# A two-layer trunk whose instruction order comes from the framework's other engine model

## The chip, the cores and the metric

The kernel runs on one core of one Trainium2 chip. The metric is the device time of one execution in microseconds (us), as the median of several runs. The engines are PE (matrix products), DVE (VectorE), ACT (ScalarE), POOL (GpSimd) and SP (which here only issues transfers). A transfer can be issued by SP, ACT or POOL; those that add into their destination are all issued by POOL in this kernel.

## The reference

The reference is a causal decoder trunk with batch 1, 512 positions, width 1024 and two layers, all in float32:

```
x = x + dilated_attention_mixer(rmsnorm(x, g_a), w_qkv, w_out)   # 3 groups x 8 heads of 128
x = x + swiglu_ffn(rmsnorm(x, g_f0), w_gate_up[0], w_down[0])    # inner width 2816
x = x + pooling_mixer(rmsnorm(x, g_p), w_in, w_group, scale)     # windows 2, 4, 8, 16
x = x + swiglu_ffn(rmsnorm(x, g_f1), w_gate_up[1], w_down[1])
return rmsnorm(x, g_final)

def swiglu_ffn(h, w_gate_up, w_down):
    gate, up = split(h @ w_gate_up)
    return (silu(gate) * up) @ w_down
```

The attention has three groups with (window, dilation) of (128, 1), (512, 4) and (2048, 16). The outputs of the three groups are merged, head by head, by a softmax over their log-sums, and a projection follows.

## The kernel before

The activations lie with features on the 128 partitions and the 512 positions along the row: x is eight tiles of 128x512 (x_5528 to x_5535 in the program's numbering). Every product is made in split float32: a matrix is written as a rounded part and a remainder, and three matmuls stand for one (L329, L330 and L332 for plain products in `Product.add`; L461, L462 and L463 in `mult`; L632 to L634 in `values12`). Weights arrive by a transfer into a `raw` tile, then ACT copies the rounded part (L92) and DVE subtracts for the remainder (L93). In a few places, the `lean` loads, ACT writes the rounded part (L146) and its negative (L147), and a transfer by POOL adds the weight itself from memory (L149); so DVE has no part in them. The rings are short: 5 `w` tiles, 4 `raw`, 2 `half`, and all accumulators share the 8 banks of PSUM (`ps`).

Most of the large products are made by Strassen's scheme with seven products for eight. `seven` does it for queries, keys and values, `chained` for the two FFN layers, where three accumulators are reused and ACT copies each out (L535, L539, L543, L551) before the next group of matmuls starts. The sums of weight blocks that the scheme needs are made by DVE (L189, L190) from the `raw` tiles. Their results are put together by DVE (L502, L508, L515, L516 in `seven`; L664 to L677 in `values12`).

The attention runs head by head, and its pieces are hung between the products of the next head. For head h: `scores0` and `scores12` make the scores; `merge` computes the weight of each group on DVE in a chain of small steps (L771 to L781), multiplies the four score blocks `s0` on DVE (L783) and the four of `s12` on ACT (L786); `turn0` has PE transpose `s0` (L802), and ACT (L806, L808) and DVE (L809) put the result in `t0`; `turn12` does the same for `s12` (L823, L828); `output` multiplies with the values (L841, L847). L610 and L850 add or scale what PE has accumulated.

Between the sub-layers stands an RMSNorm. `note` scales each x tile for the next sub-layer (L393, L394), `square` squares it on ACT (L382) and adds the squares up on DVE (L384); `rstd` sums them with PE matmuls against ones (L411), then DVE (L414) and POOL (L417) take the power, and `spread` brings the row to all partitions with PE (L424). In the last FFN each down product is added to x (L1224, or L1361 for one half of the positions). The final norm is taken in two halves of the positions, each with its own `rstd`: of the first half the five late tiles are added (L1361), squared (L1363) and summed (L1402), then L1373 scales the eight tiles and they are written. Of the second half, tiles are scaled by the norm's weights first (L1389 on ACT, L1387 on DVE), turned by PE (L1397) and scaled by the power at the end (L1437, L1439).

**What sets the order.** The Python code emits the instructions in one sequence, in which the author has interleaved the stages by hand (a planner, `pump`, walks two queues of loads and weight splits ahead of the products, and lists of hooks hang attention steps between products). The tile framework takes this sequence, builds the dependences, and lets a scheduler choose the order in which each engine will issue its instructions. That scheduler walks a model of the engines in time. The program it emits is static: each engine issues its own list in order, and an instruction that is not ready holds up all those behind it on its engine, however ready these may be. Semaphores are put in for the order chosen. Which tile of a ring a new value gets follows from the sequence as well.

In the program before, PE's order is nearly the written one: counted over all pairs of PE instructions, 6 pairs stand the other way round.

## Time and profile before

| | before |
|---|---|
| time, median of 3 runs | 1186.43 us (1184.93 to 1186.91) |
| span of the profiled execution | 1184.0 us |
| PE busy | 1175.4 us (99%), 10042 matmuls |
| DVE busy | 989.0 us (84%) |
| ACT busy | 721.7 us (61%) |
| POOL busy | 171.3 us (14%) |
| transfers | 207.57 MB, mean 175 GB/s |

The profile is of one execution, and its times count from the start of the span. Busy time is what an engine spent in its instructions; matmuls overlap, so their own durations are longer than the distance from one start to the next. A row of the timeline has the start, the busy time, the engine, the line of the kernel, the operation, its output and inputs, their shapes, how many instructions were put together, and in brackets how long the engine stood idle before it and who ended that. The heads are numbered 0 to 7: up to about 475 us the core is in the attention, then to about 786 us in the first FFN, to about 860 us in the pooling layer, and then in the second FFN.

### The profile page before, as it was taken

What the parts mean: (1) busy time and instruction counts of PE and PEld (TensorE: products, weight loads), DVE (VectorE), ACT (ScalarE), POOL (GpSimd) and SP (SyncE); (2) the same over time, 40 slices, a digit from 0 to 9 for tenths busy, and PEclk for the clock granted to TensorE, in tenths of its full rate; (3) what the DMA queues carried; (4) which work ended last, traced back from release to release, by engine and by line L of the source; (5) the groups of instructions that cost most, each with busy time, mean ns of one, the idle gap of its engine ahead of it and who ended that gap; (6) DMA issues with size and microseconds to landing.
All of it is one profiled execution on the core that took longest, in us unless ns stands there. A gap on an engine that the chain in (4) does not pass through costs nothing.

```text
span 1184.0 us, 25180 instructions
## 1 busy us (share of the span) xinstructions
PE 1175.4 (99%) x10042; PEld 1119.9 (95%) x10042; DVE 989.0 (84%) x1733; ACT 721.7 (61%) x1262; POOL 171.3 (14%) x165
## 2 busy tenths in 40 slices
PE   9999999999999999999999999999999999999997
PEld 7889999999999989889999999988889999999997
DVE  7997898889789888699988988656789998898875
ACT  6554564546455557747756775775575766676553
POOL 1101111111111002311111111122130111111100
PEclk9999999999999999999999999999999999999999
DMA  8537667666856557957777877798595777877732
GB/s 302 130 95 187 147 153 166 168 160 152 192 140 169 145 157 195 246 113 203 191 188 189 204 184 209 195 265 208 121 195 119 187 199 195 198 191 193 197 92 72
DMA packets 83766, 207.57 MB, mean 175 GB/s; under 512 B 7856, under 2 KB 13120, under 8 KB 83648
## 3 DMA queue, kind: packets, MB, share of 16 engines
q1 hardware_dynamic: 52672, 144.84, 36.9%
q0 software_dynamic: 30688, 60.83, 31.6%
q8 instruction: 78, 1.28, 0.4%
q14 instruction: 40, 0.33, 0.1%
q10 hardware_dynamic: 288, 0.29, 0.1%
HBM read 203.84 MB, written 2.10 MB: 174 GB/s over the span
## 4 chain that ended last, share of the span: by engine, by line
PE 96%; DMA 1%; issue 1%; DVE 1%; ACT 0%; POOL 0%; POOLq 0%; DVEq 0%; ACTq 0%
PE ps L461 21%; PE ps L462 20%; PE ps L463 20%; PE ps L329 7%; PE ps L330 7%; PE ps L332 7%; PE ps L928 2%; PE ps L632 2%; PE ps L633 2%; PE ps L634 2%; DMA raw<-w_outp 1%; PE ps L847 1%; PE ps L716 1%; PE ps L736 1%; PE ps L841 1%
## 5 line engine op out<-in xcount | busy, mean ns | idle before, releaser
L92 ACT ACTIVATE w<-raw 128x1024 fp32r<-128x1024 f32 x268 | 283.7, 1063 | 177.0 <-PE ps L463 73.3
L93 DVE TENSOR_TENSOR w<-raw,w 128x1024 fp32r<-128x1024 f32 x268 | 326.4, 1222 | 48.8 <-ACT w L92 44.7
L461 PE MATMUL ps<-far,w 128*128 128x256 f32 x896 | 246.5, 275 | 0.0
L462 PE MATMUL ps<-far,w 128*128 128x256 f32 x896 | 246.4, 275 | 0.0
L463 PE MATMUL ps<-far,w 128*128 128x256 f32 x896 | 246.4, 275 | 0.0
L461 PE MATMUL ps<-near,w 128*128 128x256 f32 x676 | 190.5, 282 | 0.0
L462 PE MATMUL ps<-near,w 128*128 128x256 f32 x676 | 186.9, 277 | 0.0
L463 PE MATMUL ps<-near,w 128*128 128x256 f32 x676 | 186.9, 276 | 0.0
L462 PEld LDWEIGHTS ps<-far,w 128*128 128x128 f32 x896 | 168.2, 188 | 0.1
L461 PEld LDWEIGHTS ps<-far,w 128*128 128x128 f32 x896 | 168.2, 188 | 0.1
L463 PEld LDWEIGHTS ps<-far,w 128*128 128x128 f32 x896 | 168.2, 188 | 0.0
L461 PEld LDWEIGHTS ps<-near,w 128*128 128x128 f32 x676 | 127.1, 188 | 0.5
L462 PEld LDWEIGHTS ps<-near,w 128*128 128x128 f32 x676 | 127.1, 188 | 0.0
L463 PEld LDWEIGHTS ps<-near,w 128*128 128x128 f32 x676 | 127.0, 188 | 0.0
L329 PE MATMUL ps<-near,w 128*128 128x512 f32 (+1 forms) x316 | 119.4, 379 | 0.0
L332 PE MATMUL ps<-near,w 128*128 128x512 f32 (+1 forms) x316 | 118.7, 376 | 0.0
L330 PE MATMUL ps<-near,w 128*128 128x512 f32 (+1 forms) x316 | 118.7, 376 | 0.0
L173 POOL DMA_DIRECT2D raw<-w_pair x36 | 43.6, 1210 | 291.7 <-DMA raw<-w_pair 87.3
L329 PEld LDWEIGHTS ps<-near,w 128*128 128x128 f32 x316 | 59.3, 188 | 11.0 <-ACT near L92 0.4
L332 PEld LDWEIGHTS ps<-near,w 128*128 128x128 f32 x316 | 59.3, 188 | 10.9
L330 PEld LDWEIGHTS ps<-near,w 128*128 128x128 f32 x316 | 59.4, 188 | 10.6 <-DVE near L93 0.2
L92 ACT ACTIVATE half<-rawhalf 128x512 fp32r<-128x512 f32 x84 | 52.8, 630 | 13.7 <-PE ps L463 11.8
(333 smaller groups left out, 2802.7 us busy)
## 6 DMA issues: line engine op xcount, KB each, us to landing
raw<-w_pair SPq DMA_DIRECT2D x80, 512.0 KB, 4.9
raw<-w_qkp SPq DMA_DIRECT2D x38, 512.0 KB, 4.5
raw<-w_pair POOLq DMA_DIRECT2D x36, 512.0 KB, 7.6
raw<-w_dblock SPq DMA_DIRECT2D x32, 512.0 KB, 4.7
raw<-w_qkp POOLq DMA_DIRECT2D x19, 512.0 KB, 7.5
raw<-w_v SPq DMA_DIRECT2D x18, 512.0 KB, 4.1
rawhalf<-w_pair SPq DMA_DIRECT2D x36, 256.0 KB, 5.2
raw<-w_dblock POOLq DMA_DIRECT2D x16, 512.0 KB, 7.5
```

Source lines behind the costliest of these rows:

```text
L92: nc.scalar.activation(hi, v, AF.Copy)
L93: nc.vector.tensor_tensor(lo, v, hi.bitcast(F32), op=OP.subtract)
L173: nc.gpsimd.dma_start(self.b.rearrange("p (a c) -> p a c", a=2), self.src[:, None, 3 * n:].to_broadcast([P, 2, n]), accum_op=OP.add)
L329: nc.tensor.matmul(self.p[:, cols], w[0][:, s], mh[:, cols], start=self.done == 0, stop=False)
L330: nc.tensor.matmul(self.p[:, cols], w[0][:, s], ml[:, cols], start=False, stop=False)
L332: nc.tensor.matmul(self.p[:, cols], w[1][:, s], mh[:, cols], start=False, stop=self.done == self.n)
L461: nc.tensor.matmul(dst, w.t[0][:, c], th, start=k == 0 and not on, stop=False, skip_group_check=on)
L462: nc.tensor.matmul(dst, w.t[0][:, c], tl, start=False, stop=False, skip_group_check=on)
L463: nc.tensor.matmul(dst, w.t[1][:, c], th, start=False, stop=k == n - 1, skip_group_check=on)
L632: nc.tensor.matmul(o, mh, wh, start=k == 0, stop=False)
L633: nc.tensor.matmul(o, mh, wl, start=False, stop=False)
L634: nc.tensor.matmul(o, ml, wh, start=False, stop=k == K2 - 1)
```

## The change

One argument is added where the framework is opened:

```diff
     out = nc.dram_tensor("out", (2, D * H2), F32, kind="ExternalOutput").ap()
-    with tile.TileContext(nc) as tc:
+    with tile.TileContext(nc, schedule_with_timeline_sim=True) as tc:
         trunk(tc, **aps, outT=out[0].rearrange("(k p s) -> k p s", k=KC, p=P),
```

The scheduler then walks its other engine model when it chooses the next instruction of each engine. Nothing that is computed changes, and no instruction of PE, DVE, ACT or POOL is added or dropped. What changes is the order on each engine, and with it the semaphores. Of the 9284 instructions on PE's list 4754 stand at another place, up to 60 places earlier and 50 later, and the pairs that stand against the written order go from 6 to 45348. On ACT 729 instructions moved, on DVE 1190, on POOL 16, and on SP 34 transfers. Three of the places follow.

The first is DVE at the merge of head 5's scores, between the products of head 6 (around 322 to 333 us). `s0_3631` are the scores that PE transposes next; `co_4164`, `mx_4161`, `ex_4162` and `dd_4163` are the small tiles of the chain that leads to them; `w_4238`, `w_4255` and `half_4324` are splits of weights; `raw_4117` gets the sums of weight blocks; `qk00_4081` and `qk01_4082` are results of head 6's products. Before:

```order
L776 TENSOR_TENSOR ex_4162<-st_3629,mx_4161 128x16
L778 TENSOR_TENSOR dd_4163<-ex_4162,st_3629 128x16
L779 TENSOR_TENSOR mx_4161<-dd_4163 128x8
L780 RECIPROCAL mx_4161<-mx_4161 128x8
L781 TENSOR_TENSOR co_4164<-ex_4162,mx_4161 128x8
L783 TENSOR_SCALAR s0_3631<-s0_3631,co_4164 128x160 x4
L502 TENSOR_TENSOR qk00_4081<-ps_4084,first_4099 128x16x16x2
L93 TENSOR_TENSOR w_4238<-raw_4117,w_4238 128x1024
L508 TENSOR_TENSOR sums_4100<-ps_4086,qk00_4081 128x256 x2
L93 TENSOR_TENSOR w_4255<-raw_4118,w_4255 128x1024
```

The same place now, from the row behind L776 on:

```order
L93 TENSOR_TENSOR w_4238<-raw_4117,w_4238 128x1024
L778 TENSOR_TENSOR dd_4163<-ex_4162,st_3629 128x16
L502 TENSOR_TENSOR qk00_4081<-ps_4084,first_4099 128x16x16x2
L189 TENSOR_TENSOR raw_4117<-raw_4117,raw_4118 128x512
L779 TENSOR_TENSOR mx_4161<-dd_4163 128x8
L508 TENSOR_TENSOR sums_4100<-ps_4086,qk00_4081 128x256 x2
L190 TENSOR_TENSOR raw_4117<-raw_4117 128x512
L93 TENSOR_TENSOR w_4255<-raw_4118,w_4255 128x1024
L780 RECIPROCAL mx_4161<-mx_4161 128x8
L515 TENSOR_TENSOR qk01_4082<-ps_4085,sums_4100 128x16x16x2
L516 TENSOR_TENSOR qk00_4081<-sums_4100,ps_4085 128x8x16x2
L93 TENSOR_TENSOR half_4324<-rawhalf_4119,half_4324 128x512
```

After the last of these rows come L781 and the four L783. Between the first step of the small chain and the scaling of `s0` there now stand two whole weight splits, a half one, two sums of weight blocks and five results of products.

The second place is the change from the first FFN to the pooling layer (around 768 to 806 us). On PE the last down products of the FFN accumulate in `ps_9851`, `ps_9861`, `ps_9894` and so on, with the weights `w_9701` (two products), `w_9719` (two), `w_9789` and `w_9809`; each needs one operand that comes last. Before, the end of the first two products reads:

```order
L329 MATMUL ps_9851<-near_82,w_9701 128x512
L329 MATMUL ps_9861<-near_82,w_9701 128x512
L329 MATMUL ps_9894<-near_82,w_9719 128x512
L330 MATMUL ps_9851<-near_82,w_9701 128x512
L332 MATMUL ps_9851<-near_82,w_9701 128x512
L330 MATMUL ps_9861<-near_82,w_9701 128x512
L332 MATMUL ps_9861<-near_82,w_9701 128x512
L330 MATMUL ps_9894<-near_82,w_9719 128x512
```

Now the four products that follow have been begun ahead of it, and it reads:

```order
L332 MATMUL ps_9982<-near_82,w_9809 128x512
L329 MATMUL ps_9851<-near_82,w_9701 128x512
L329 MATMUL ps_9861<-near_82,w_9701 128x512
L329 MATMUL ps_9894<-near_82,w_9719 128x512
L329 MATMUL ps_9913<-near_82,w_9719 128x512
L330 MATMUL ps_9851<-near_82,w_9701 128x512
L332 MATMUL ps_9851<-near_82,w_9701 128x512
L330 MATMUL ps_9861<-near_82,w_9701 128x512
L332 MATMUL ps_9861<-near_82,w_9701 128x512
```

Seven down products are now open at once, with only their last operand missing, and `w_9701` is read until their end. At the same place ACT has this order before, where `sq_10024` is the last square of the norm and `w_10085` and `w_10095` are weights of the pooling layer:

```order
L393 ACTIVATE h_10021<-x_5535,nrm_75 128x512
L382 ACTIVATE sq_10024<-x_5535 128x512
L146 ACTIVATE w_10085<-raw_9886 128x1024
L147 ACTIVATE w_10085<-w_10085 128x1024
L146 ACTIVATE w_10095<-raw_9930 128x1024
```

and now:

```order
L382 ACTIVATE sq_9998<-x_5534 128x512
L146 ACTIVATE w_10085<-raw_9886 128x1024
L146 ACTIVATE w_10095<-raw_9930 128x1024
L382 ACTIVATE sq_10024<-x_5535 128x512
L147 ACTIVATE w_10085<-w_10085 128x1024
```

The last square stands behind the first copies of two weights.

The third place is DVE in the last microseconds. `ps_14490` holds the spread row of the first half's norm, `total_14534` is the sum of squares that the second half's norm needs. Before, the L1373 stand among the steps of the second half:

```order
L1373 SCALAR_TENSOR_TENSOR x_5531<-x_5531,nrm_75,ps_14490 128x256
L1361 TENSOR_TENSOR x_5534<-x_5534,ps_14517 128x256
L1402 TENSOR_TENSOR total_14513<-total_14481,sq_14511 128x256
L1373 SCALAR_TENSOR_TENSOR x_5532<-x_5532,nrm_75,ps_14490 128x256
L1402 TENSOR_TENSOR total_14534<-total_14513,sq_14532 128x256
L1361 TENSOR_TENSOR x_5535<-x_5535,ps_14536 128x256
```

Now all eight stand in a row ahead of them; the last of the eight and what follows:

```order
L1373 SCALAR_TENSOR_TENSOR x_5534<-x_5534,nrm_75,ps_14490 128x256
L1373 SCALAR_TENSOR_TENSOR x_5535<-x_5535,nrm_75,ps_14490 128x256
L1361 TENSOR_TENSOR x_5534<-x_5534,ps_14517 128x256
L1361 TENSOR_TENSOR x_5535<-x_5535,ps_14536 128x256
L1387 TENSOR_SCALAR ends_14336<-x_5535,nrm_75 128x256
L1402 TENSOR_TENSOR total_14534<-total_14513,sq_14532 128x256
```

`x_5534` and `x_5535` of the second half, and the sum after them, moved behind the whole output of the first half.

## The prediction

> **What bounds the kernel now.** I read the busy times and the chain of waits on the page first, then the waits of PE, then the table by windows.
>
> ```profile
> span 1184.0 us, 25180 instructions
> PE 1175.4 (99%) x10042; PEld 1119.9 (95%) x10042; DVE 989.0 (84%) x1733; ACT 721.7 (61%) x1262; POOL 171.3 (14%) x165
> PE 96%; DMA 1%; issue 1%; DVE 1%; ACT 0%; POOL 0%; POOLq 0%; DVEq 0%; ACTq 0%
> PE ps L908 <- DVE idle L905: 1.2, 1, 1.2
> PE ps L841 <- ACT t L808: 0.8, 1, 0.8
> 540.00:570.00 30.00, 30.00 (x267) 30.00 (x267) 28.66 (x55) 22.60 (x41) 3.22 (x4) 1.00 0.72 185
> 1170.00:1184.00 14.00, 7.64 (x95) 7.23 (x93) 7.69 (x20) 4.22 (x10) 1.70 (x4) 0.93 0.43 151
> ```
>
> PE is busy 99% of the span and makes up 96% of the chain. It waits for another engine twice: 1.2 us at the very start and 0.8 us once in head 7. The window rows (length, then busy time of PE, weight load, DVE, ACT and POOL, the granted clock, the transfers) show PE idle for 6.4 us in the last 14 us. So a better order can give back a few us at the ends, while a worse one can hold PE up anywhere: PE issues in order, and the rest of its list slips with the instruction that waits. The number of matmuls is the same, so the forecast is the sum of new waits of PE. For each instruction of PE that waits for a changed order I set when its input comes against when PE reaches it. The sum is made against the span of 1184.0 us; the median is 2.4 us above that.
>
> **The FFN layers (475 to 770 and 860 to 1150 us): nothing.** In the window 540 to 570 one product matmul starts every 30/267 = 0.112 us and PE has no gap. The new order puts the next accumulator's first matmuls between two uses of one bank, so ACT's copies out of PSUM get later deadlines. PE did not wait there, so that is worth nothing. DVE, 28.66 of 30 us busy, does the same work there; its cover of 1.3 us per 30 us is thin, but the splits of weights are 5 to 7 us ahead of their use.
>
> **Head 0, about 78 us.** PE transposes `s0` (L802) once DVE has scaled it (L783).
>
> ```profile
> 75.55 0.94 DVE L783 TENSOR_SCALAR s<-s,co 128x160 f32<-128x160 f32 x4
> 76.82 0.69 DVE L610 TENSOR_TENSOR qk<-ps,row 128x512 f32<-128x512 f32 x1 [0.33 <-PE ps L332]
> 78.84 1.23 DVE L93 TENSOR_TENSOR w<-raw,w 128x1024 fp32r<-128x1024 f32 x1
> 79.98 1.25 DVE L809 STREAM_TRANSPOSE t<-s 32x128 f32<-32x128 f32 x4
> ...
> 77.43 1.04 ACT L92 ACTIVATE w<-raw 128x1024 fp32r<-128x1024 f32 x1
> ...
> 78.04 0.60 PE L802 MATMUL ps<-ident,s 128*128 128x128 f32 x4
> ```
>
> Before, `s0` was done at 76.5 and PE came at 78.04. Now DVE has L610, which cannot start before 76.8 (it waits for PE), then L780, then the L93 whose rounded part ACT delivers at 78.47 here, then L781, an L189 and the L783. Two neighbours on DVE start 1.14 us apart behind an L93 (78.84 to 79.98) and 0.6 behind a 128x512 step. ACT now comes to that L92 about 0.5 us sooner, so L93 starts at 77.9, and 77.9 + 1.14 + 0.2 + 0.6 + 0.94 = 80.8. PE waits 80.8 - 78.0 = **2.8 us**; 3.3 if ACT is not sooner.
>
> **Head 5, about 328 us**, the place shown in the change:
>
> ```profile
> 322.90 0.28 DVE L776 TENSOR_TENSOR ex<-st,mx 128x16 f32<-128x16 f32 x1
> 324.31 0.94 DVE L783 TENSOR_SCALAR s<-s,co 128x160 f32<-128x160 f32 x4
> 325.17 0.69 DVE L502 TENSOR_TENSOR qk<-ps,first 128x512 f32<-128x512 f32 x1
> 325.77 1.22 DVE L93 TENSOR_TENSOR w<-raw,w 128x1024 fp32r<-128x1024 f32 x1
> 326.90 0.75 DVE L508 TENSOR_TENSOR sums<-ps,qk 128x256 f32<-128x256 f32 x2
> 329.30 0.41 DVE L516 TENSOR_TENSOR qk<-sums,ps 128x256 f32<-128x256 f32 x1
> ...
> 323.34 1.04 ACT L92 ACTIVATE w<-raw 128x1024 fp32r<-128x1024 f32 x1
> ...
> 328.31 0.60 PE L802 MATMUL ps<-ident,s 128*128 128x128 f32 x4
> ```
>
> The four L783 ended at 325.25, 3 us ahead of PE. Now they stand behind the splits. The first L93 cannot start before ACT's L92 (323.34 + 1.04, some 0.2 sooner if ACT takes it ahead of L777), at about 324.2. Behind it stand, each by its distance to the next (its busy time less the 0.09 by which neighbours overlap, as 325.17 to 325.77 shows): L93 twice 1.13, a half L93, L502, L189, L190 and L515 each 0.6, two L508 0.67, L516 0.34, four small steps 0.6 in all, L783 0.94: 2.26 + 3.0 + 0.67 + 0.34 + 0.6 + 0.94 = 7.8. So `s0` is done at 324.2 + 7.8 = 332.0 and PE waits 332.0 - 328.3 = **3.65 us**. If everything up to the first L93 ran without waiting (323.1), it would be 2.6.
>
> **Head 7, about 424 us.**
>
> ```profile
> 415.46 0.93 DVE L783 TENSOR_SCALAR s<-s,co 128x160 f32<-128x160 f32 x4
> 420.42 1.23 DVE L93 TENSOR_TENSOR w<-raw,w 128x1024 fp32r<-128x1024 f32 x1 [1.70 <-ACT w L92]
> ...
> 419.33 1.06 ACT L92 ACTIVATE w<-raw 128x1024 fp32r<-128x1024 f32 x1 [5.30 <-DMA raw<-w_outp]
> ...
> 423.62 0.60 PE L802 MATMUL ps<-ident,s 128*128 128x128 f32 x4
> ...
> 429.57 0.49 PE L841 MATMUL ps<-t,v 128*128 128x128 f32 x2 [0.81 <-ACT t L808]
> ```
>
> Now L781 and L783 are queued behind that L93 of 420.42, which waits for a transfer. If it starts at 419.8 to 420.4, there follow the L93 (1.14), eight steps of 128x512 (L673, L677, L1028, two halves, one more operand, L189, L190) of 0.6, L781 and L783 (1.1): 426.8 to 427.4. PE waits 3.2 to 3.8 us. But PE's old stall (its last matmul starts at 428.38, the next at 429.57, 1.2 us where 0.2 is the rule) goes, since ACT's L806 and L808 then end before PE comes. Net **2.2 us**.
>
> **The change of layer, 770 to 806 us.**
>
> ```profile
> 776.58 1.06 ACT L146 ACTIVATE w<-raw 128x1024 fp32r<-128x1024 f32 x1 [1.99 <-PE ps L332]
> 778.67 1.05 ACT L147 ACTIVATE w<-w 128x1024 fp32r<-128x1024 f32 x1
> 795.35 0.62 ACT L382 ACTIVATE sq<-x 128x512 f32<-128x512 f32 x1
> ...
> 780.08 0.86 POOL L149 DMA_DIRECT2D w<-w_pin  x1 [5.87 <-ACT w L147]
> ...
> w<-w_pin POOLq DMA_DIRECT2D x4, 512.0 KB, 8.3
> ...
> 796.14 0.69 DVE L384 TENSOR_TENSOR sq<-sq 128x512 f32<-128x512 f32 x1
> ...
> 793.83 0.39 PE L329 MATMUL ps<-near,w 128*128 128x512 f32 x1
> 794.06 0.39 PE L330 MATMUL ps<-near,w 128*128 128x512 f32 x1
> ...
> 803.44 0.43 PE L411 MATMUL ps<-ones,sq 128*32 128x1 f32 x32
> ```
>
> The first row is the first copy of `w_9882`, which may be written only when PE has read `w_9701` for the last time. Two matmuls of 128x512 start 0.227 us apart (793.83, 794.06; 0.23 by these two, 0.227 over a longer row of them). In the new list 73 of them stand between the last product with `w_9701` and L411: 803.4 - 73 x 0.227 = 786.9, ten us later than before. From there: L146 1.06, two L393/L382 pairs and another L146 (about 3.3, against 1.0 between the two copies before), L147 1.06, 0.4 to POOL's issue, and the transfer's 8.3: 786.9 + 14.1 = 801.0. PE needs the remainder of `w_9882` 34 matmuls ahead of L411 in its new list, at 803.4 - 7.7 = 795.7. That is a wait of 5.3; with a transfer of 7 us and ACT's copies as close together as before it is 2, with one of 10.4 it is 7.5. I take **5.5**, since ACT has more in its way than the two pairs. Behind it, the last square: before it was done at 796.8 and L411 did not wait. Now it follows the first copies of `w_10085` and `w_10095`, and the second of these waits for the last matmul that reads `w_9882`, directly ahead of L411. So after that end come L146 0.95, L382 0.62, L384 0.69 and the hand-overs, some 0.7: **3.0 us** by which PE waits at L411, wherever that then stands. Together 8.5, between 5 and 10.5.
>
> **The tail, from 1168 us.**
>
> ```profile
> 1168.71 0.31 PE L411 MATMUL ps<-ones,total 128*32 128x1 f32 x16
> 1169.27 0.42 ACT L1363 ACTIVATE sq<-x 128x256 f32<-128x256 f32 x1 [0.94 <-DVE x L1361]
> 1169.59 0.50 ACT L1389 ACTIVATE ends<-x,nrm 128x256 f32<-128x256 f32 x1
> 1172.06 1.26 DVE L1373 SCALAR_TENSOR_TENSOR x<-x,nrm,ps 128x256 f32<-128x256 f32 x3
> 1176.41 0.31 PE L411 MATMUL ps<-ones,total 128*32 128x1 f32 x16
> ```
>
> On ACT one L1389, which needs the second half's L1361 (1168.82 + 0.42), now stands ahead of three squares of the first half: 1169.3 + 4 x 0.33, then DVE's last sum 0.43: the first L411 moves from 1168.7 to 1171.2. The second L411 needs `total_14534`, behind eight L1373 at 0.39 (3.1 us), and these need the L424, which now stands behind 24 matmuls of the second half's down products instead of 18, with 5 more inside it: at 0.12 each and 0.36 for L411 itself it ends 4.5 us after L411, at 1175.7. So 1175.9 + 3.1 + two L1361, L1387 and L1402 with their hand-overs (1.5) = 1180.5, against 1176.41. What follows L411 is the same chain as before. The tail adds **4.1 us**, the 2.5 of the first L411 included. If the tail's engines overlap better it is 2.5; the start (30 to 60 us) and all other merges have input in time and add nothing.
>
> **Sum:** 2.8 + 3.65 + 2.2 + 8.5 + 4.1 = 21.3; 1184.0 + 21.3 = 1205.3 us of span; with the 2.4 to the median **1207.7 us**. Low ends: 2.6 + 2.6 + 1.5 + 5 + 2.5 = 14.2 (1200.6); high ends: 3.3 + 4 + 3 + 10.5 + 5 = 25.8 (1212).
>
> **The rivals.** *A, no change* (1186.4): the waits are absorbed. For it: outside the ends PE waited once in 1184 us, so the order of the others was far ahead of it. Against: slack is a matter of place; `s0` was 1.5, 3 and 7 us ahead, and it is set back 4, 7 and 11. It would hold if DVE's and ACT's lists reached these places sooner, but DVE is 84% busy and its rows there wait for PE's and ACT's own products. *B, faster* (1183.5): only the stalls of before go, 0.8 to 1.2 in head 7, and up to 1.7 more at the ends, and none of the new waits comes. For it: the FFN's margins get wider. Point of decision: the three L802 and the L411 at 803 would show no idle. *C, the clock* (1211): a PE that stands still loses granted clock. The row of the last 14 us shows 0.93 where PE idles 6.4 us, and all others 1.00; 0.07 x 14 = 1.0 us per 6.4 us idle, so 21 us of idle would cost 3.3 more. Against: that window holds idle time behind PE's last matmul, where a low clock costs nothing. [...] *D, DVE in the FFN* (1225): with a list that runs ahead in splits, DVE (28.66 of 30) delays results and PE idles by 0.4 us or so in each of the 44 pairs of gate and up products, 17 us on top of the forecast. Against: the results' deadlines got later, not sooner.
>
> **How the numbers follow.** Forecast 0.66, C 0.15, D 0.09, A 0.06, B 0.04. A measurement of this kernel can tell about 0.2%, 2.4 us, from no change. Slower holds the forecast, C and D, 0.90; same most of A and a bit of B, 0.06; faster 0.04. The range 1194 to 1217 holds the forecast's own bounds (1200.6 to 1212), C, and the case that one of the two large terms (layer change 8.5, tail 4.1) is wholly hidden; D, A and B are outside.
>
> **What would show it.** PE's waits after the change should name L802 three times with 2.5 to 4 us each, with L783 as the one waited for; an L332 that waits for the transfer of `w_pin` by 4 to 7 us at about 805; L411 waiting on DVE's L384 by 3 us behind it; and the two L411 of the tail 2 to 3 us and 1 to 2 us later relative to the last down product. The windows of both FFNs should have PE busy throughout. The forecast is wrong if PE's idle time is under 10 us more than before, or if it lies in the FFN windows.

## The result and the profile after

The changed kernel takes 1213.36 us (median; 1212.13 to 1214.95) against 1186.67 us (1184.93 to 1187.17) for the kernel before: 1.023 times as long, 95% interval 1.0216 to 1.0245. The forecast was 1207.7 us with a range of 1194 to 1217.

The profiled execution has a span of 1212.8 us, 28.8 more than before. These are lines of its page, its waits of PE, and its windows (length, busy time of PE, weight load, DVE, ACT and POOL, granted clock, which is the share of its full clock that PE was given, and transfers):

```profile
span 1212.8 us, 25135 instructions
PE 1186.5 (98%) x10042; PEld 1128.6 (93%) x10042; DVE 986.9 (81%) x1733; ACT 707.9 (58%) x1262; POOL 170.1 (14%) x165
PE 93%; issue 3%; DMA 2%; DVE 1%; ACT 0%; POOL 0%; DVEq 0%; POOLq 0%; ACTq 0%
...
PE ps L802 <- DVE s L783: 8.7, 3, 3.6
PE ps L411 <- DVE sq L384: 2.9, 1, 2.9
PE ps L411 <- DVE total L1402: 2.4, 1, 2.4
PE ps L332 <- DMA w<-w_pin: 2.1, 1, 2.1
PE ps L1397 <- ACT ends L1389: 1.3, 1, 1.3
PE ps L332 <- DMA w<-w_down: 1.0, 1, 1.0
...
60.00:120.00 60.00, 57.28 (x513) 53.61 (x513) 50.01 (x90) 31.62 (x66) 7.63 (x7) 0.97 0.49 119
570.00:770.00 200.00, 200.00 (x1767) 200.00 (x1766) 177.53 (x301) 130.33 (x235) 24.21 (x20) 1.00 0.75 195
810.00:840.00 30.00, 25.06 (x130) 20.06 (x130) 14.75 (x27) 18.35 (x26) 6.63 (x8) 0.89 0.97 228
1170.00:1200.00 30.00, 27.57 (x217) 25.78 (x216) 14.26 (x29) 10.80 (x23) 1.10 (x2) 0.94 0.00 1
```

PE now waits at L802 in three heads, at L411 in the norm behind the first FFN, at L411 and L1397 in the tail, and twice at an L332 for a transfer into a `w` tile. In 200 us of the first FFN (570 to 770) it has no gap. PE's busy time is 11 us longer for the same 10042 matmuls, and the granted clock is 0.97, 0.89 and 0.94 in the windows that hold waits. All but two of the waits, that at L1397 and that for the transfer from `w_down`, are the forecast's; the longer matmuls are not in its sum.

How the two go together shows in head 0. The timeline of PE, of the changed kernel:

```profile
78.88 0.28 PE L463 MATMUL ps<-near,w 128*128 128x256 f32 x1
81.88 0.63 PE L802 MATMUL ps<-ident,s 128*128 128x128 f32 x4 [2.72 <-DVE s L783]
82.52 0.42 PE L462 MATMUL ps<-near,w 128*128 128x256 f32 x1
82.73 0.41 PE L463 MATMUL ps<-near,w 128*128 128x256 f32 x1
...
85.72 0.32 PE L462 MATMUL ps<-near,w 128*128 128x256 f32 x1
85.88 0.28 PE L463 MATMUL ps<-near,w 128*128 128x256 f32 x1
85.99 0.28 PE L461 MATMUL ps<-tx,w 128*128 128x256 f32 x1
```

Behind the wait of 2.72 us one matmul of 128x256 follows the other by 0.21 us for 3.4 us (82.4 to 85.8), and by 0.115 again after that. Sixteen matmuls at 0.1 us more each are 1.6 us lost.

The delay against the profile of before, read where the same instruction of PE starts in both:

| place | before | after | delay |
|---|---|---|---|
| head 0, L802 and L823 | 78.04, 82.58 | 81.88, 88.05 | +3.8, +5.5 |
| head 5, L802 and L823 | 328.31, 331.49 | 338.29, 343.12 | +10.0, +11.6 |
| head 7, L802 and L841 | 423.62, 429.57 | 437.93, 442.97 | +14.3, +13.4 |
| L411 behind the attention | 477.71 | 490.81 | +13.1 |
| L411 behind the first FFN | 803.44 | 824.70 | +21.3 |
| L411 behind the pooling layer | 859.36 | 882.24 | +22.9 |
| the two L411 of the tail | 1168.71, 1176.41 | 1194.24, 1205.61 | +25.5, +29.2 |

From 13.1 at 490 us the delay moves only at the change of layer, and from 22.9 at 882 us only in the tail: in 600 us of FFN nothing is lost or gained.

### The profile page after: what moved, and what is told of

It is laid out like the page before. It is cut to its first block, busy times and chain, and to the rows that moved or that the text cites. A ratio compares the mean times of both kernels' runs of the same rounds, so it can differ in the third digit from the quotient of the medians.

```text
span 1212.8 us, 25135 instructions
## 1 busy us (share of the span) xinstructions
PE 1186.5 (98%) x10042; PEld 1128.6 (93%) x10042; DVE 986.9 (81%) x1733; ACT 707.9 (58%) x1262; POOL 170.1 (14%) x165
## 3 DMA queue, kind: packets, MB, share of 16 engines
q8 instruction: 78, 1.28, 0.4%
## 4 chain that ended last, share of the span: by engine, by line
PE 93%; issue 3%; DMA 2%; DVE 1%; ACT 0%; POOL 0%; DVEq 0%; POOLq 0%; ACTq 0%
PE ps L461 20%; PE ps L462 20%; PE ps L463 20%; PE ps L329 7%; PE ps L332 7%; PE ps L330 7%; PE ps L632 2%; PE ps L633 2%; PE ps L634 2%; PE ps L928 2%; PE ps L847 1%; PE ps L716 1%; DMA w<-w_down 1%; DMA x<-xN 1%; PE ps L736 1%
## 5 line engine op out<-in xcount | busy, mean ns | idle before, releaser
L92 ACT ACTIVATE w<-raw 128x1024 fp32r<-128x1024 f32 x268 | 282.5, 1062 | 168.9 <-PE ps L463 48.9
L93 DVE TENSOR_TENSOR w<-raw,w 128x1024 fp32r<-128x1024 f32 x268 | 325.6, 1219 | 55.8 <-ACT w L92 54.9
L462 PE MATMUL ps<-far,w 128*128 128x256 f32 x896 | 243.6, 275 | 0.0
L461 PE MATMUL ps<-far,w 128*128 128x256 f32 x896 | 242.0, 275 | 0.0
L463 PE MATMUL ps<-far,w 128*128 128x256 f32 x896 | 241.6, 275 | 0.0
L461 PE MATMUL ps<-near,w 128*128 128x256 f32 x676 | 190.1, 284 | 0.0
L461 PEld LDWEIGHTS ps<-far,w 128*128 128x128 f32 x896 | 166.5, 188 | 0.2
L462 PEld LDWEIGHTS ps<-near,w 128*128 128x128 f32 x676 | 128.3, 190 | 0.1
L463 PEld LDWEIGHTS ps<-near,w 128*128 128x128 f32 x676 | 128.2, 190 | 0.0
L461 PEld LDWEIGHTS ps<-near,w 128*128 128x128 f32 x676 | 127.6, 190 | 0.4
L332 PE MATMUL ps<-near,w 128*128 128x512 f32 (+1 forms) x316 | 120.8, 383 | 3.1 <-DMA w<-w_pin 2.1
L92 ACT ACTIVATE half<-rawhalf 128x512 fp32r<-128x512 f32 x84 | 52.7, 629 | 57.1 <-PE ps L463 55.3
L332 PEld LDWEIGHTS ps<-near,w 128*128 128x128 f32 x316 | 60.9, 193 | 14.9 <-DMA w<-w_pin 2.5
L330 PEld LDWEIGHTS ps<-near,w 128*128 128x128 f32 x316 | 60.9, 193 | 11.4 <-DVE near L394 0.4
L329 PEld LDWEIGHTS ps<-near,w 128*128 128x128 f32 x316 | 60.6, 193 | 10.8
```

What stands on the lines that cost most here:

```text
L92: nc.scalar.activation(hi, v, AF.Copy)
L93: nc.vector.tensor_tensor(lo, v, hi.bitcast(F32), op=OP.subtract)
L329: nc.tensor.matmul(self.p[:, cols], w[0][:, s], mh[:, cols], start=self.done == 0, stop=False)
L330: nc.tensor.matmul(self.p[:, cols], w[0][:, s], ml[:, cols], start=False, stop=False)
L332: nc.tensor.matmul(self.p[:, cols], w[1][:, s], mh[:, cols], start=False, stop=self.done == self.n)
L461: nc.tensor.matmul(dst, w.t[0][:, c], th, start=k == 0 and not on, stop=False, skip_group_check=on)
```

## The experiments

**How an order is put back in one stretch.** The order of each engine can be written down as a list and held: each instruction of the list is tied behind the one before it on its engine, without a wait. For a stretch, the list follows the changed kernel up to a point, takes everything that the kernel before issues up to a second point, in its order, and then goes on with the order of the changed kernel; the two points are called its seams. Waits, tiles and sums stay those that the data needs.

```diff
     with tile.TileContext(nc, schedule_with_timeline_sim=True) as tc:
         trunk(tc, **aps, outT=out[0].rearrange("(k p s) -> k p s", k=KC, p=P),
               outR=out[1].rearrange("(s d) -> s d", d=D))
+        pins(tc)
...
+def pins(tc):
+    same = mybir.DependencyInfo(mybir.DependencyClass.NoSync, mybir.DependencyReason.DATA)
+    traced = {x.name: x for x in tc.nc.cur_bb.bb.instructions}
+    for engine, text in ORDER.items():
...
+                if prev is not None:
+                    tc.add_manual_dep(x, prev, same, reason="order")
+                prev = x.name
```

Seven of the kernels below differ from the changed kernel or from the one before only in ORDER.

**The three merges.** ORDER has the sequence of before from 58 to 100, 312 to 345 and 400 to 440 us.

> The changed kernel, with the order of before on all engines in three stretches only (58 to 100, 312 to 345 and 400 to 440 us of before), where heads 0, 5 and 7 are merged. My theory: the three waits of PE at L802 go (2.9 + 3.7 + 2.5, less the 0.9 that the change had saved in head 7) and with them the half-speed stretches behind two of them (1.6 + 1.7), 11.5 us in all: 1201.9 us. Rival one, the slow clock belongs to the new program and not to its waits: only the 8.2 us of waiting go, 1205.2. Rival two, the wait is only passed on, because DVE's whole queue is late there: PE waits elsewhere behind it, 1209 or more.

Measured: 1201.97 us (1.0138 of before, 1.0121 to 1.0155). My theory gave 1201.9, the rivals 1205.2 and 1209 or more. Of the three waits at L802 one of 1.1 us is left, in head 0, some 20 us behind the stretch's first seam; the wait for L808 in head 7 is back at 0.9. No slow stretch is left in the attention (the granted clock is 1.00 in each window from 0 to 770 us), so rival one falls; no new wait of PE stands behind the three places, so rival two falls too. That the median meets the theory to 0.1 us is luck in part: the wait left in head 0 was not in it, and the four runs lie between 1199.64 and 1203.43.

**The change of layer.** ORDER has the sequence of before from 750 to 815 us.

> The changed kernel, with the order of before on all engines only from 750 to 815 us of before (the change from the first FFN to the pooling layer). My theory: the waits for the transfers into w (1.2 and 2.2 us) and of L411 (3.05) go, and the half-speed stretches behind the last two (1.7 + 1.6): 9.8 us, 1203.6 us. Rival, the clock is not a matter of the waits: 6.4 us, 1207.0.

Measured: 1204.74 us (1.0159, 1.0144 to 1.0174); theory 1203.6, rival 1207.0. The waits of L332 for transfers and of L411 for L384 are gone, and from 360 to 1150 us each window shows a clock of 1.00, so the slow stretches went with them. The time alone, 1.1 us above the theory and 2.3 below the rival with runs from 1203.55 to 1206.83, would not decide.

**The tail.** ORDER has the sequence of before from 1135 us on.

> The changed kernel, with the order of before on all engines only from 1135 us of before to the end. My theory: the wait of the first L411 (2.6 us), the half-speed stretch behind it (1.7) and the 1.6 us by which the second half's norm comes later go: 5.9 us, 1207.5 us. Rival, the clock is not a matter of the waits: 4.2 us, 1209.2.

Measured: 1206.2 us (1.0175, 1.0154 to 1.0196); theory 1207.5, rival 1209.2. It is lower than both; the four runs lie between 1204.45 and 1210.33, and the profile, that of the lowest, shows one reason. In this run head 0 has its wait of 2.7 us, as in the changed kernel, and no slow stretch behind it; and the clock of 0.98 from 770 to 870 us, where the waits are 1.7 us for `w_9882` and 2.9 us at L411, is that of one stretch, where the changed kernel has two. Windows of this kernel:

```profile
77.00:81.00 4.00, 1.53 (x13) 1.32 (x11) 3.66 (x10) 3.57 (x8) 0.00 (x0) 1.00 0.00 0
81.00:85.00 4.00, 3.76 (x33) 3.79 (x34) 3.03 (x10) 3.06 (x9) 0.00 (x0) 1.00 0.00 0
```

and of the changed kernel, where PE got 23 matmuls done in the four microseconds after the wait, at 0.57 of the clock, instead of 33:

```profile
78.00:82.00 4.00, 1.28 (x11) 1.11 (x11) 3.66 (x10) 3.37 (x7) 0.00 (x0) 1.00 0.00 0
82.00:86.00 4.00, 4.00 (x23) 4.00 (x23) 2.67 (x9) 3.09 (x8) 0.00 (x0) 0.57 0.00 0
```

So the same wait may bring the slow stretch or not; what decides was not shown.

**All five stretches.** ORDER has the sequence of before in all of them.

> The changed kernel with the order of before in all five stretches together; the rest, both FFN layers among it, keeps the new order. My theory: the three gains add up to 27.2 us, and what is left is the 0.9 us at the start: 1186.2 to 1187.5 us, the same as before within what can be told. Rival, the FFN's new order costs or gives something by itself: outside 1184 to 1189.

Measured: 1190.37 us (1189.37 to 1190.72), 1.0036 of before (1.0022 to 1.0049): 23.0 of the 26.7 us are gone, 3 to 4 us less than I had expected to go. Its waits:

```profile
PE ps L461 <- ACT first L535: 1.2, 2, 1.0
PE ps L802 <- DVE s L783: 1.2, 1, 1.2
PE ps L461 <- ACT sums L551: 0.5, 1, 0.5
PE ps L841 <- ACT t L808: 0.3, 1, 0.3
```

The longest L535 wait is at 1139 us and that for L551 at 752, right behind the seams at 1135 and 750; neither stands in the changed kernel or in the one before. The one at L802 is in head 0: DVE is 3.0 us late at L746 behind the seam at 58 and still 2.6 late at L783. None of these waits is followed by a slow stretch: the granted clock is 1.00 in each window from 0 to 1150 us. The time lies outside 1184 to 1189, where the rival had it, but the rival's mechanism does not show. Read at the same instructions of PE, the delay against before stays at 0.7 us from 478 to 749 us and at 2.1 from 776 to 1130, the two FFN layers in their new order, and rises by 1.3 at the seam at 750 and by 1.6 at that at 1135. The seams, which I had left out of the sum, make 2.9 of the 3.7 us; no kernel without seams was tried.

**One late place alone.** The kernel before, with the changed kernel's order from 312 to 345 us only. PE's rows are the same as before; on DVE this is the first place shown in the change.

> The kernel before, with the new order on all engines in one stretch only (312 to 345 us, where head 5 is merged); PE's order is the same there in both, so what is new is DVE's order, a few rows of ACT and two of SP. My theory: PE waits 3.7 us at head 5's L802 and then runs 3.4 us at half speed, which is another 1.7: 5.4 us over before, 1191.3. Rival one, the slow clock of the changed kernel has another cause: 3.7 us over before, 1189.6. Rival two, one late place alone is caught up, since the rest of DVE's order is that of before: within 1 us of before, 1186.9 or less.

Measured: 1191.11 us, 1.0046 of before (1.003 to 1.0063), 5.3 us more; theory 1191.3, rivals 1189.6 and 1186.9. The waits of PE and three windows of this kernel, in the row's order wait, start, slow stretch:

```profile
PE ps L802 <- DVE s L783: 3.5, 1, 3.5
...
328.00:332.10 4.10, 0.58 (x6) 0.41 (x5) 4.03 (x12) 1.45 (x5) 0.00 (x0) 1.00 0.36 132
332.10:333.10 1.00, 0.99 (x9) 1.00 (x10) 0.96 (x4) 0.64 (x3) 0.00 (x0) 1.00 0.56 193
333.10:336.60 3.50, 3.50 (x19) 3.50 (x19) 1.84 (x6) 2.93 (x7) 1.23 (x1) 0.52 0.35 56
```

The clock falls not in the wait, and not with its end, but 1 us later, when PE is at full work again, and for 3.4 us. One changed place in an otherwise unchanged kernel makes its wait and its slow clock.

**Waits of chosen length, a miss.** The kernel before, with more work on DVE at the merges:

```diff
+                for i in range(MORE[h]): nc.vector.tensor_scalar(s0, s0, 1.0, None, op0=OP.mult)
                 for b in (1, 2, 3, 0):
                     nc.vector.tensor_scalar(s0[:, b], s0[:, b], co[:, 0, b:b + 1], None, op0=OP.mult)
```

> The kernel before, in which DVE multiplies the scores of a head by one several times more (4, 8, 9, 9, 11, 6 and 15 times for heads 0 to 6; about 0.75 us each) ahead of L783, so that PE waits at L802 for a chosen time: about 1.5, 2.3, 2.3, 3.1, 3.9, 1.5 and 6.8 us. My theory: a wait has a step in it: behind waits of some 1.3 us and less PE keeps its pace, behind waits of 2.7 and more it runs 3.4 us at half speed, however long the wait was, so that each costs 1.7 us more; between 1.3 and 2.7 either is possible. Rival, the loss grows with the wait (0.45 us lost for each us waited, from 1.65 behind 3.7): 0.7 behind 1.5 us, 3.1 behind 6.8 us.

> As the kernel with more multiplications, with other counts (5, 7, 8, 8, 9, 7 and 8 for heads 0 to 6), so that the waits lie between 1.5 and 2.4 us. [...] Rival, the loss grows with the wait: 0.7 to 1.1 us behind each of the seven.

Measured: 1188.19 and 1186.48 us (one run each), with 1185.85 for before on the same chip. PE waited nowhere at the transposes of `s0` (L802, one line further down in these kernels): multiplying by one ahead of the scaling needs only `s0`, which is ready long before its weight is, so the multiplications went into DVE's idle time. They tell nothing of the clock. They tell that DVE has room in the attention: in the second kernel 52 steps more (1785 against 1733, 1010.9 us busy against 989.0) cost 0.6 us. With 62 more, in the first, PE waited 0.9 and 0.8 us at two other places (L740 for L515, L769 for L757).

**Waits of chosen length.** The same line, behind the loop:

> The kernel before, in which DVE multiplies the scores of heads 0 to 6 by one several times more (2, 4, 5, 5, 6, 4 and 8 times), this time behind L783, between the scaling and PE's L802; other steps of DVE come between them, so that one costs about 1.4 us, and PE waits about 1.3, 1.9, 2.6, 3.4, 4, 2.5 and 6.8 us. My theory: the loss has a step: behind waits of 1.3 us and less PE keeps its pace, behind 2.7 and more it runs 3.4 us at half speed and loses 1.7 us, however long the wait was; between, either. Rival, the loss grows with the wait (0.45 us for each us waited, from 1.65 behind 3.7): 0.6 behind 1.3 us, 3.1 behind 6.8 us.

> As the kernel beside it with other counts (3, 5, 4, 4, 5, 3 and 5 multiplications behind L783 for heads 0 to 6), so that the waits lie about between 1.1 and 3.3 us. My theory: each wait is followed by the whole 1.7 us of loss, or by none, none under about 1.3 us. Rival, the loss grows with the wait: 0.5 to 1.5 us behind each.

Measured: 1200.23 and 1192.46 us (one run each; 1185.57 before). The waits came out shorter than planned: 0.3 to 3.9 us, and none in heads where there was more room; in the second kernel none was over 1.3, so the lengths that it was made for were not reached. Behind those of 0.88, 1.12 and 1.28 us PE kept its pace (and in the second kernel the granted clock is 0.999 over the run); behind the two longest of the first kernel it did not. A window of the wait and the four microseconds behind it, first for the wait of 2.12 us, then for the one of 3.86:

```profile
276.00:279.00 3.00, 0.91 (x9) 0.71 (x7) 3.00 (x6) 0.60 (x2) 0.00 (x0) 1.00 0.43 77
279.00:283.00 4.00, 3.96 (x21) 3.99 (x22) 3.92 (x11) 2.81 (x8) 0.00 (x0) 0.57 0.20 51
...
383.00:388.00 5.00, 1.16 (x11) 0.97 (x10) 5.00 (x11) 0.85 (x2) 0.00 (x0) 1.00 0.21 38
388.00:392.00 4.00, 3.98 (x22) 4.00 (x23) 3.40 (x10) 3.16 (x8) 0.17 (x1) 0.60 0.48 160
```

21 and 22 matmuls in 4 us: both lost the same, though one wait was nearly twice the other. The rival, a loss that grows with the wait, falls.

**The two halves of the change of layer.** The changed kernel with the order of before from 750 to 786 us (the down products finish one after the other), and with that from 790 to 815 us (the last square stands ahead of the copies; ACT's rows against the changed kernel below).

```
-L146 ACTIVATE w_10085<-raw_9886 128x1024
-L146 ACTIVATE w_10095<-raw_9930 128x1024
 L382 ACTIVATE sq_10024<-x_5535 128x512
+L146 ACTIVATE w_10085<-raw_9886 128x1024
+L147 ACTIVATE w_10085<-w_10085 128x1024
+L146 ACTIVATE w_10095<-raw_9930 128x1024
```

> The changed kernel with the order of before only from 750 to 786 us of before: the last down products of the first FFN finish one after the other again, so that w_9701 is free early; the last square (sq_10024) still stands behind the first copies of w_10085 and w_10095 on ACT. My theory: the two waits for transfers into w (1.2 and 2.2 us) go with the half-speed stretch behind the second (1.7), 5.1 us, 1208.3 us; L411 still waits 2.9 us for L384, with 1.6 of slow clock behind it. Rival, the late w_9882 is behind the late square too: L411's wait goes as well, 1203.7 us.

Measured: 1209.4 us (1.0194, 1.0177 to 1.0212); theory 1208.3, rival 1203.7. Both waits for transfers are gone and L411's stands as it was; L461 waits 0.7 us behind the seam.

> The changed kernel with the order of before only from 790 to 815 us of before: seven down products are still open at once, but ACT makes the last square ahead of the copies of w_10085 and w_10095, and PE's pooling products take w_9882 in the order of before, 1.4 us later. My theory: L411's wait goes with the slow stretch behind it (2.9 + 1.6 us), and the wait for w_9882 shrinks to under 1 us, so that no slow stretch follows it (2.2 + 1.7 less up to 1): 7.4 to 8.4 us, 1205 to 1206 us; the wait of 1.2 us at about 782 stays. Rival, the square is late because w_9882 is: L411 still waits 2 us or more, and the time stays above 1209.

Measured: 1210.57 us (1.0209, 1.0192 to 1.0227). I had expected 1205 to 1206. PE's waits in this stretch are now others:

```profile
PE ps L329 <- ACT near L393: 2.0, 2, 1.5
PE ps L332 <- DMA w<-w_down: 1.9, 1, 1.9
...
PE ps L330 <- DVE near L394: 0.9, 3, 0.3
```

L411's wait and that for `w_9882` are gone, so the late square is a matter of the order and not of `w_9882`, and the rival falls, though the time is above the 1209 that it gave. Most of the time did not come back: ACT now takes the squares and the copies between the L393, and PE waits for these, the next operands, 2.9 us in five pieces, with 1.6 us of slow clock behind them. With the seven down products finishing together, both orders of ACT that were tried keep PE waiting for something; the new order had put the L393 first.

## Why the prediction was right, and where it was not

The direction and the places were right, and so was the cause of the waits; a second cost behind them was left out of the sum. The time is above the forecast's own high end of 1212 us; it lies inside the range because the range was drawn to hold rival C too. Term by term (waits are given as the shift of PE's start):

| step of the prediction | forecast | measured |
|---|---|---|
| FFN layers | 0 | 0; PE busy 200.00 of 200 us |
| head 0 | 2.8 | 2.9 |
| head 5 | 3.65 | 3.7 |
| head 7, net | 2.2 | 2.5 - 0.9 = 1.6 |
| layer change, waits for transfers | 5.5 | 2.2, and 1.2 not foretold |
| layer change, L411 | 3.0 | 3.05 |
| tail | 4.1 | 2.65 + 2.0 - 0.4 = 4.2 |
| start, heads 1 to 4 | 0 | 0.9 + 0.7 |
| slow clock behind the waits | 0 (rival C: 3.3) | 1.6 + 1.7 + 1.6 + 1.6 + 1.7 = 8.2 |

The waits that I had summed, with the one not foretold, came to 18.9 us against 21.3. The start's 0.9 us is not the order's: with the same order up to 58 us, the kernel with all five stretches put back is level with before at 27 us.

**DVE's order at the merges.** Of head 0 the chain came as forecast, all 0.9 us later:

```profile
77.78 0.69 DVE L610 TENSOR_TENSOR qk<-ps,row 128x512 f32<-128x512 f32 x1
78.93 1.23 DVE L93 TENSOR_TENSOR w<-raw,w 128x1024 fp32r<-128x1024 f32 x1 [0.34 <-ACT w L92]
80.07 0.16 DVE L781 TENSOR_TENSOR co<-ex,mx 128x8 f32<-128x8 f32 x1
80.80 0.93 DVE L783 TENSOR_SCALAR s<-s,co 128x160 f32<-128x160 f32 x4
```

**The transfer of `w_9882`.** The step that set its start was right: the first copy 10 us later, the second 4.2 us behind it (forecast 4.4), POOL's issue 0.4 behind that.

```profile
801.06 1.06 ACT L146 ACTIVATE w<-raw 128x1024 fp32r<-128x1024 f32 x1 [6.36 <-PE ps L332]
805.24 1.05 ACT L147 ACTIVATE w<-w 128x1024 fp32r<-128x1024 f32 x1
806.64 0.86 POOL L149 DMA_DIRECT2D w<-w_pin  x1 [15.60 <-ACT w L147]
812.18 0.50 PE L332 MATMUL ps<-near,w 128*128 128x512 f32 x1 [2.05 <-DMA w<-w_pin]
```

The mis-sized term is the transfer: PE goes on 5.5 us after the issue, where I took the 8.3 that four such transfers had as their median in the profile of before. My low bound for this term, 2 us, was what came, and not the 4 to 7 named as the sign. Why the transfer was quicker stays open. A wait of 1.0 us (1.2 of shift) at 782 us for another accumulating transfer I had not priced.

**The tail** has the same sum by another split. Its working holds a slip: the spread row was put 4.5 us behind the first L411, but the parts named for it (29 matmuls at 0.12 and 0.36) make 3.8. With 0.2 to the first L1373 that is 4.7 in the sum; measured, L1373 starts 6.3 us behind L411, 1.7 of it slow clock. So the 4.7 was about right and its list of parts incomplete. The second L411 was late as foretold, eight L1373 in a row ahead of it, but part of it was that PE's L1397 waited 1.3 us for an L1389, which waits behind the same eight for L1361:

```profile
1200.51 3.22 DVE L1373 SCALAR_TENSOR_TENSOR x<-x,nrm,ps 128x256 f32<-128x256 f32 x8
1203.65 0.74 DVE L1361 TENSOR_TENSOR x<-x,ps 128x256 f32<-128x256 f32 x2
```

**The step that failed** is that the sum counted a wait of PE as the wait alone. Rival C named the clock and was held apart as a case of its own at 0.15; it was not a rival but a part of the forecast's own path. I priced it at 3.3 us, from a window at the end of the program where idle time costs nothing. The runs show five stretches of 1.6 or 1.7 us lost each, 8.2 us together, four of them behind waits of 2.0 to 2.9 us. With it the sum is 21.3 + 8.2 = 29.5 against 28.8 of span; that it comes so near is luck, since two further misses, 2.4 us too much for the waits and 1.6 too little for the start and heads 1 to 4, nearly cancel. Rivals A, B and D fall: the waits came at all places named, L411 and the three L802 have idle time, and PE has no gap in the FFN.

## What to carry to other kernels

Where one engine is busy all the time (here PE, 99% of the span before) and issues in order, an order is judged by the few places where that engine needs a chain of small steps from others; ask what now stands ahead of the chain's last step in each engine's list, and when those rows can start, before asking how busy the engines are on the mean. A row whose own input is late is the worst to have ahead: it holds all behind it. At head 7 of the changed kernel DVE stood idle for 2.44 us ahead of an L93 that waited for ACT's L92; L781 and the four L783 stand behind it, and PE waited 2.37 us at L802. And price a wait of the matrix engine as the wait and what may come behind it: in the changed kernel five of the six waits between 2.05 and 3.57 us were followed by a stretch of slow matmuls that lost 1.6 or 1.7 us, the one of 2.37 us was not.

## What the runs showed of the hardware

The loss in slow matmuls behind a wait did not grow with the wait. In the profile of the changed kernel, with PE's idle time as the trace has it (left out are PE's first wait, at the very start, and the last 10 us, where PE runs out of work; from 1200 us to the end the granted clock is 0.84):

| PE's wait | PE idle | stretch at a granted clock of 0.50 behind it |
|---|---|---|
| L332 for `w_down`, at 782 us | 1.00 us | none |
| L332 for `w_pin`, at 812 us | 2.05 us | 812.82 to 816.23 us |
| L802, head 7, at 438 us | 2.37 us | none |
| L411 of the tail, at 1194 us | 2.43 us | 1195.12 to 1198.53 us |
| L802, head 0, at 82 us | 2.72 us | 82.37 to 85.78 us |
| L411 behind the first FFN, at 825 us | 2.89 us | 826.48 to 829.89 us |
| L802, head 5, at 338 us | 3.57 us | 338.37 to 341.78 us |

Each stretch was 3.41 us long at half of the full clock, which is 1.7 us lost, whatever the wait had been; it began between 0.1 and 1.8 us after PE went on. These are the windows of the wait in head 0 and of the stretch behind it:

```profile
78.96:82.37 3.41, 0.69 (x7) 0.52 (x6) 3.41 (x9) 2.41 (x6) 0.00 (x0) 1.00 0.00 0
82.37:85.78 3.41, 3.41 (x19) 3.41 (x18) 2.30 (x8) 2.87 (x8) 0.00 (x0) 0.50 0.00 0
```

In the experiments a slow stretch stood behind the wait of 3.53 us in the kernel with one late place, and behind those of 2.12 and 3.86 us in the first kernel with waits of chosen length; none stood behind the waits of up to 1.2 us in the kernel with all five stretches of the order put back. Of head 0's same wait of 2.7 us, the changed kernel has a slow stretch behind it and the kernel with the tail of before has none. The short waits at the change of layer in the last kernel, five pieces of 0.28 to 1.52 us with matmuls between them, were followed by one. What sets the waits with a slow stretch apart from those without was not shown.

So the same kernel may differ from one run to the next by 1.7 us for each wait that falls one way or the other; this is an estimate from the two outcomes of head 0's wait. The four times of the kernel with the tail of before, 1204.45, 1205.71, 1206.69 and 1210.33 us, go with their granted clocks of 0.996, 0.995, 0.994 and 0.991 over the run; only the first of them has a profile.
